# A two-layer decoder trunk on one core: the order of plain and seven-product matmuls in the down projection, the third weight sum, and the place of the gates

## The chip, the cores and the metric

The kernel runs on 1 core of one Trainium2 chip, as one program. The metric is the device time of one execution in microseconds. Three runs of the kernel before gave a median of 2934.0 us (2933.38 to 2938.09).

TensorE (PE) does the matmuls and writes them to PSUM; VectorE (DVE) and ScalarE (ACT) do the elementwise work; GpSimd (POOL) does little here but issue some transfers; SyncE (SP) issues most transfers. Every engine takes its own instructions in the order of the program.

## What is computed

Two decoder layers on 256 tokens of width 2048, in float32. Layer 0 mixes with a gated DeltaNet and a latent attention side by side, layer 1 with retention. Each layer then has a gated feed-forward part with a short convolution, which is where most of this change lies, and a gated embedding:

```python
def conv_ffn(hn, w_up, conv_w, conv_b, w_down):
    u = causal_dwconv(hn @ w_up, conv_w) + conv_b
    gate, up = jnp.split(u, 2, axis=-1)
    return (jax.nn.silu(gate) * up) @ w_down
```

`w_up` is 2048 x 11264 and `w_down` 5632 x 2048. The DeltaNet needs two small gates per token and head, from 16 columns of its input projection:

```python
    beta = jax.nn.sigmoid(b.astype(f32)).transpose(0, 2, 1)
    g = (-jnp.exp(A_log.astype(f32)) * jax.nn.softplus(a.astype(f32) + dt_bias.astype(f32))
         ).transpose(0, 2, 1)
```

## The kernel before

**Split precision.** Every product of two float32 matrices is made of three products of float32r parts: high x high, low x high, high x low. A block of weights is loaded into one of four `raw` buffers of 1 MB (L167). `cut` (L186, L187) makes its high part on ScalarE by a rounding copy, and its low part on VectorE by a subtraction, in halves of 128x1024; there are four buffers each for the high halves (`hi`) and the low ones (`lo`). TensorE then runs the two products with the high part (in a "high step") and the one with the low part (in a "low step"). So a weight passes SyncE, ScalarE, VectorE and TensorE in turn, and every stage can only be as far ahead as it has buffers.

**The feed-forward part.** The 44 blocks of 128 hidden units are taken in groups: 4, then five groups of 8. For a group, `up` makes the hidden units (`gemm_b`, L259 and L264, 48 steps for a group of 8), convolves and gates them, and leaves them split in tiles `xg`. `down` multiplies a finished group with its rows of `w_down` and adds the result to the residual `h`. `down` of one group runs while `up` of the next one does: both are generators that give up their turn at each `yield`, and `ffn` takes 6 steps of `up` (`LAG`), and from then on 0.9 steps of `down` (`SHARE`) for one of `up`.

**The two ways of `down`.** The output has 2048 columns, four blocks of 512. For the first and the last group all four are plain matrix products (`gemm_a`, L288, L289 and L294): 6 steps a block, 24 matmuls of 512 columns for each load of 1 MB. For the four groups between, columns 1024 to 2047 are plain (12 steps), and columns 0 to 1023 are done by `seven`: tokens, hidden units and these 1024 columns are halved each, so that hidden units, weights and results fall into four quarters, and the four quarters of the result come from seven products of sums of quarters instead of eight products of quarters. There are four such groups in each layer, eight in all, and 56 products.

**One product** (`product`, L423, L424 and L428) has 3 steps: two high steps of 4 matmuls and a low step of 4 + 4. Its left side is a sum of quarters of the hidden units (`Forms`), made ahead on VectorE, or a quarter of them. Its right side is either a quarter of `w_down`, loaded by SyncE into a `raw` buffer (`fresh`), or a sum of two to four quarters. Such a sum is made by the transfers themselves: SyncE writes the first quarter (`put`, L396), and POOL issues a transfer that adds the next one to what is there (`plus`, L400). Both come as two transfers of 512 KB. One running sum, `run_t`, lies in two `xg` tiles of its own and serves three products, with one more quarter added before the second and the third; it can only be added to when the product before has been cast. The other sum, `t3`, the third weight sum of the change's title, lies in a `raw` buffer.

**The order within a group before.** `down` first calls `seven` once, which issues `put` and `plus` for the first running sum. Then come the 12 plain steps, then the 21 steps of the seven products. `t3` is begun after the second product, and used by the sixth. PSUM has four banks for `down` (`pb`): a plain block takes two, and `seven` holds three from its start on.

**Who sets the order.** The program is written with tiles; a scheduler at build time simulates the engines and lays down each engine's order, in general after the order of the text. `tc.issue_after(ins)` ties the instructions written under it behind `ins`, where both are on one engine; `last_cast` is the latest rounding copy of `cut` on ScalarE.

**The gates.** The input projection starts with 3 x 368 columns (`g3` 0 to 2, `gemm_a` with loads of 4 x 368). After the first 368 the 16 gate columns are there; `gates` (L568 to L602) computes `beta` and the decay with small steps on ScalarE and VectorE, among them two loads of a function table on ScalarE. It ends in two small matmuls of cumulative sums (L598, L599). `low_rank` normalises the compressed query, and `rope_tables` (L470 to L495) makes angles on VectorE.

## Time and profile before

| what | us |
|---|---|
| median of three runs | 2934.0 |
| the profiled execution, its time | 2930.12 |
| its span, first to last instruction | 2928.3 |
| PE busy | 2878.1 (98%) |
| DVE busy | 2042.5 (70%) |
| ACT busy | 1532.7 (52%) |
| POOL busy | 141.1 (5%) |

The mean granted clock of TensorE is 0.995 of full speed over the span. The DMA engines moved 570.88 MB, 195 GB/s on average. The page gives busy time of each engine, the chain of work that ended last, and groups of instructions by line, with the idle time ahead of them and what ended it. A group's `x16` is sixteen instructions. In rows of the timeline a bracket like `[1.27 <-ACT hi L186]` says that the engine sat idle for 1.27 us before this instruction, and that ScalarE's instruction of line 186 on a tile `hi` ended it. Rows of windows give, after the window's length, the busy time of PE, PEld (weight loads), DVE, ACT and POOL with the number of instructions, then the granted clock, the mean busy share of the DMA engines and GB/s.

### The profile page before, as it was taken

To read this page: it belongs to the slowest core of one execution; us is meant where nothing else is said; L and a number is where in the kernel's file an instruction comes from. 1 tells how busy PE (TensorE), PEld (TensorE's weight loads), DVE (VectorE), ACT (ScalarE), POOL (GpSimd) and SP (SyncE) were. 2 spreads that over 40 slices of the span, in tenths; PEclk is the share of its full clock that TensorE was granted. 3 is DMA by queue.
4 is the path that set the end of the run, shared out by engine and by line. 5 is a ranking of instruction groups with operands and counts; after the bars stand their busy time and mean duration, and the time that the engine had idled before them with its cause. 6 is when DMAs were issued, how large, how long until landed. Compare 5 with 4: busy or idle time off the path is not lost.

```text
span 2928.3 us, 38655 instructions
## 1 busy us (share of the span) xinstructions
PE 2878.1 (98%) x15076; PEld 2469.8 (84%) x15076; DVE 2042.5 (70%) x2874; ACT 1532.7 (52%) x2185; POOL 141.1 (5%) x132
## 2 busy tenths in 40 slices
PE   8999999999999999999999999999999999999998
PEld 8899988888888888888888888888888887888887
DVE  6878867776868787756665565565677777786865
ACT  6666655554545555554444443444545555555554
POOL 0111100001000000000000000000000000000000
PEclk9999999999999999999999999999999999999999
DMA  6444455568778778555555555555556778777854
GB/s 217 137 141 126 127 165 194 187 198 227 228 208 246 216 232 235 182 191 190 177 188 181 194 180 187 183 182 187 185 188 216 219 227 226 219 216 229 235 180 150
DMA packets 414393, 570.88 MB, mean 195 GB/s; under 512 B 11009, under 2 KB 267137, under 8 KB 414209
## 3 DMA queue, kind: packets, MB, share of 16 engines
q1 hardware_dynamic: 393376, 530.05, 55.4%
q0 software_dynamic: 17408, 33.56, 6.7%
q10 hardware_dynamic: 3424, 4.79, 0.5%
q8 instruction: 118, 1.93, 0.3%
q14 instruction: 67, 0.54, 0.1%
HBM read 566.26 MB, written 2.10 MB: 194 GB/s over the span
## 4 chain that ended last, share of the span: by engine, by line
PE 91%; DMA 3%; DVE 3%; ACT 2%; issue 1%; SPq 0%; POOL 0%; ACTq 0%; POOLq 0%; DVEq 0%
PE pa L259 27%; PE pa L264 14%; PE pa L288 10%; PE pa L289 10%; PE pa L294 10%; DMA raw<-in_l_ffn_w_down_dram 3%; PE pb L289 3%; PE pb L288 3%; PE pb L294 3%; PE pb L698 2%; DVE lo L187 1%; PE pb L424 1%; PE pb L423 1%; PE pb L428 1%; ACT hi L186 1%; PE pb L308 1%
## 5 line engine op out<-in xcount | busy, mean ns | idle before, releaser
L187 DVE TENSOR_TENSOR lo<-raw,hi 128x1024 fp32r<-128x1024 f32 (+3 forms) x1140 | 1194.2, 1075 | 605.2 <-ACT hi L186 493.1
L186 ACT CAST hi<-raw 128x1024 fp32r<-128x1024 f32 (+3 forms) x1140 | 1007.8, 930 | 976.6 <-PE pa L289 327.4
L259 PE MATMUL pa<-xg,hi 128*128 128x512 f32 x3840 | 946.9, 393 | 0.0
L259 PEld LDWEIGHTS pa<-xg,hi 128*128 128x128 f32 x3840 | 714.2, 189 | 143.5 <-DVE xg L313 0.3
L288 PE MATMUL pa<-hi,xg 128*128 128x512 f32 (+1 forms) x1348 | 523.3, 388 | 7.2 <-ACT hi L186 7.1
L289 PE MATMUL pa<-hi,xg 128*128 128x512 f32 (+1 forms) x1348 | 520.8, 387 | 0.3 <-DVE xg L313 0.2
L264 PEld LDWEIGHTS pa<-xg,lo 128*128 128x128 f32 x3840 | 490.2, 191 | 16.4
L264 PE MATMUL pa<-xg,lo 128*128 128x256 f32 x3840 | 501.9, 283 | 0.0
L294 PE MATMUL pa<-lo,xg 128*128 128x512 f32 (+1 forms) x1348 | 332.7, 387 | 0.0
L288 PEld LDWEIGHTS pa<-hi,xg 128*128 128x128 f32 x1348 | 253.7, 188 | 56.9 <-ACT hi L186 7.7
L289 PEld LDWEIGHTS pa<-hi,xg 128*128 128x128 f32 x1348 | 253.8, 188 | 49.0 <-DVE xg L313 0.8
L294 PEld LDWEIGHTS pa<-lo,xg 128*128 128x128 f32 x1348 | 249.8, 188 | 47.5
L1033 DVE SCALAR_TENSOR_TENSOR t<-t,fp,t 128x255 f32<-128x255 f32 (+1 forms) x352 | 157.0, 480 | 57.0 <-ACT t L1031 54.2
L1031 ACT ACTIVATE t<-t,fp 128x256 f32<-128x256 f32 x176 | 96.1, 593 | 84.5 <-DVE t L274 84.4
L271 ACT COPY t<-pa 128x512 f32<-128x512 f32 x128 | 74.9, 585 | 117.0 <-PE pa L264 107.6
L289 PE MATMUL pb<-hi,xg 128*128 128x512 f32 x348 | 135.9, 391 | 0.0
L288 PE MATMUL pb<-hi,xg 128*128 128x512 f32 x348 | 135.8, 390 | 0.0
L400 POOL DMA_DIRECT2D xg<-in_l_ffn_w_down_dram x48 | 58.0, 1207 | 1198.3 <-DMA xg<-in_l_ffn_w_down_dram 481.9
L156 POOL TENSOR_TENSOR small<-small,mhalf 128x1 f32<-128x1 f32 (+2 forms) x38 | 28.6, 753 | 1372.1 <-DVE small L1198 622.6
L272 DVE TENSOR_TENSOR t<-t,pa 128x512 f32<-128x512 f32 x128 | 87.0, 680 | 2.2 <-ACT t L271 2.2
L294 PE MATMUL pb<-lo,xg 128*128 128x512 f32 x348 | 86.5, 389 | 0.0
L313 DVE SCALAR_TENSOR_TENSOR xg<-pb,par,xg 128x256 fp32r<-128x256 f32 x136 | 59.8, 479 | 35.8 <-ACT xg L312 35.0
(280 smaller groups left out, 2236.8 us busy)
## 6 DMA issues: line engine op xcount, KB each, us to landing
raw<-in_l_ffn_w_up_dram SPq DMA_DIRECT2D x176, 1024.0 KB, 5.2
raw<-in_l_w_in_dram SPq DMA_DIRECT2D x128, 1024.0 KB, 5.1
raw<-in_l_ffn_w_down_dram SPq DMA_DIRECT2D x56, 1024.0 KB, 5.2
raw<-in_l_w_out_dram SPq DMA_DIRECT2D x44, 1024.0 KB, 5.1
raw<-in_l_ffn_w_down_dram SPq DMA_DIRECT2D x64, 512.0 KB, 5.9
raw<-in_l_ple_gate_dram SPq DMA_DIRECT2D x32, 1024.0 KB, 5.1
xg<-in_l_ffn_w_down_dram POOLq DMA_DIRECT2D x48, 512.0 KB, 7.1
xg<-in_l_ffn_w_down_dram SPq DMA_DIRECT2D x16, 512.0 KB, 6.6
```

The lines of the kernel that those rows point to most:

```text
L186: last_cast[0] = A.copy(vo(hi)[:, c], vi(rk)[:, c])
L187: V.tensor_sub(vo(lo)[:, c], vi(rk)[:, c], vo(hi)[:, c].bitcast(F32))
L259: last_mm[0] = T.matmul(ps[:, j], wh, x2, start=first, stop=False)
L264: last_mm[0] = T.matmul(ps[:, j, :S], lo[k][:, j * P : (j + 1) * P], xr(tiles, c * 8 + k)[1], start=False, stop=c == 1 and k == 7)
L271: A.copy(u, ps[:, :, S:])
L272: V.tensor_add(u, u, ps[:, :, :S])
L288: T.matmul(o[i], xh, hi[k], start=begin and k0 + k == 0, stop=False)
L289: last_mm[0] = T.matmul(o[i], xw, hi[k], start=False, stop=False)
L294: last_mm[0] = T.matmul(o[i], xl(tiles, k0 + k, i)[0], lo[k], start=False, stop=end and k0 + k == nkb - 1)
L313: V.scalar_tensor_tensor(t[:, kk, 1], pk, g, t[:, kk, 0].bitcast(F32), op0=ALU.mult, op1=ALU.subtract)
L1031: A.activation(y[:, j], u[:, j], AF.Identity, scale=fc(ct + 176), bias=fc(ct + 264))
L1033: V.scalar_tensor_tensor(y[:, j, lag:], u[:, j, : S - lag], fc(ct + (2 - lag) * 88), y[:, j, lag:], op0=ALU.mult, op1=ALU.add)
```

## The change

There are four edits.

- `down` takes plain products and the seven products in turns over the whole group: one plain step, two steps of `seven`, and so on. `seven` is still called once ahead for its first sum. `SHARE` goes from 0.9 to 0.85.
- In `seven` the product of `left(0)` is no longer kept in PSUM to have the fourth product added: it is subtracted from `h12` by itself, one more subtraction on VectorE for each group. Two banks are in use at a time instead of three.
- `t3` is begun after the fourth product instead of the second.
- `gates` and `low_rank(cq)` are tied behind the last cast on ScalarE.

```diff
--- before.py
+++ after.py
@@ -32,7 +32,7 @@
 PSA = 2
 PSB = 4
 LAG = 6
-SHARE = 0.9
+SHARE = 0.85
 RATES = [1.7, 1.1, 1.1, 0.95, 2.8]
 D = 2048
 S = 256
@@ -433,27 +433,32 @@
         put(run_t, 0, 0)
         plus(run_t, 0, 1)
         yield
-        A_, B_, C_ = pb(), pb(), pb()
-        yield from product(C_, forms.left(0), run_t, True)
-        V.tensor_sub(h22, h22, C_)
+        one = pb()
+        yield from product(one, forms.left(0), run_t, True)
+        V.tensor_sub(h22, h22, one)
+        V.tensor_sub(h12, h12, one)
         plus(run_t, 1, 1)
-        yield from product(A_, x(0, 0), fresh(0, 0), True)
-        V.tensor_add(h11, h11, A_)
+        acc = pb()
+        yield from product(acc, x(0, 0), fresh(0, 0), True)
+        V.tensor_add(h11, h11, acc)
+        one = pb()
+        yield from product(one, x(1, 0), fresh(1, 0), True)
+        V.tensor_add(h11, h11, one)
+        yield from product(acc, forms.left(1), run_t, False)
+        V.tensor_sub(h12, h12, acc)
+        plus(run_t, 1, 0)
         t3 = slab()
         put(t3, 0, 1)
         plus(t3, 1, 1)
-        yield from product(B_, x(1, 0), fresh(1, 0), True)
-        V.tensor_add(h11, h11, B_)
-        yield from product(A_, forms.left(1), run_t, False)
-        V.tensor_sub(h12, h12, A_)
-        plus(run_t, 1, 0)
-        yield from product(C_, forms.left(3), fresh(1, 1), False)
-        V.tensor_sub(h12, h12, C_)
-        yield from product(A_, forms.left(2), t3, False)
-        V.tensor_sub(h22, h22, A_)
-        V.tensor_add(h21, h21, A_)
-        yield from product(B_, x(1, 1), run_t, True)
-        V.tensor_add(h21, h21, B_)
+        one = pb()
+        yield from product(one, forms.left(3), fresh(1, 1), True)
+        V.tensor_sub(h12, h12, one)
+        yield from product(acc, forms.left(2), t3, False)
+        V.tensor_sub(h22, h22, acc)
+        V.tensor_add(h21, h21, acc)
+        one = pb()
+        yield from product(one, x(1, 1), run_t, True)
+        V.tensor_add(h21, h21, one)
 
     def put_split(t, k, n, src):
         A.copy(t[:, k : k + n, 0], src)
@@ -620,8 +625,9 @@
             nc.sync.dma_start(cst, a["cst"][:, :N_CST])
             V.tensor_copy(posf, posi)
         if g3 == 2:
-            gates()
-            low_rank(cq)
+            with tc.issue_after(last_cast[0].ins):
+                gates()
+                low_rank(cq)
             cqT = []
             later(lambda: None, lambda: None, lambda: cqT.extend(gained(cq, C_QN)))
             rope_tables(cst[:, C_IMLA : C_IMLA + 1], cos_t, sin_t, cst[:, C_SIGN : C_SIGN + 1])
@@ -1050,16 +1056,26 @@
 
         def down(g0, g1, tiles, forms):
             r0, nk = g0 * P, g1 - g0
-            if forms is not None:
-                fast = seven(w_dn, r0, 0, tiles, forms)
-                next(fast)
-            for c in range(0 if forms is None else 2, CG):
-                ps = [pb() for _ in range(NH)]
-                yield from gemm_a(w_dn, r0, nk, c * 512, 512, tiles, ps)
-                for i in range(NH):
-                    V.tensor_add(h[i][c], h[i][c], ps[i])
-            if forms is not None:
-                yield from fast
+
+            def plain(cols):
+                for c in cols:
+                    ps = [pb() for _ in range(NH)]
+                    yield from gemm_a(w_dn, r0, nk, c * 512, 512, tiles, ps)
+                    for i in range(NH):
+                        V.tensor_add(h[i][c], h[i][c], ps[i])
+
+            if forms is None:
+                yield from plain(range(CG))
+                return
+            fast = seven(w_dn, r0, 0, tiles, forms)
+            next(fast)
+            slow = plain(range(2, CG))
+            while next(slow, fast) is not fast:
+                yield
+                for _ in range(2):
+                    if next(fast, slow) is not slow:
+                        yield
+            yield from fast
 
         groups = [(max(g - 4, 0), g + 4) for g in range(0, NFT, 8)]
         prev = None
```

What the build makes of it at three places follows (tile names with their numbers; a number tells one buffer's content from another).

**The gates, on ScalarE**, behind the copies out of the first 368 columns (L547 before, L552 now). `small` tiles are the gates', `hi` are halves of weights. Before:

```order
L547 ACTIVATE slab_79<-pa_15_144,small_58_378 128x16
L547 ACTIVATE t2_61_383<-pa_15_144,small_58_378 128x352
L569 ACTIVATE small_89_561<-small_89_561 128x16
L574 ACTIVATE small_90_566<-small_90_566 128x16
L581 ACTIVATE small_93_574<-small_92_572 128x16
L590 ACT_TABLE_LOAD
L590 ACTIVATE small_97_583<-small_94_576 128x16
L594 ACT_TABLE_LOAD
L594 ACTIVATE small_98_587<-alog_388 128x8
L186 CAST hi_68_403<-raw_67_401 128x368 x2
L186 CAST hi_70_409<-raw_67_401 128x368 x2
L186 CAST hi_75_445<-raw_74_443 128x368 x2
```

Now:

```order
L552 ACTIVATE slab_79<-pa_15_144,small_58_378 128x16
L552 ACTIVATE t2_61_383<-pa_15_144,small_58_378 128x352
L186 CAST hi_68_403<-raw_67_401 128x368 x2
...
L186 CAST hi_87_527<-raw_84_519 128x368 x2
L574 ACTIVATE small_89_561<-small_89_561 128x16
L579 ACTIVATE small_90_566<-small_90_566 128x16
L586 ACTIVATE small_93_574<-small_92_572 128x16
L186 CAST hi_109_643<-raw_108_641 128x368
L595 ACT_TABLE_LOAD
L595 ACTIVATE small_97_583<-small_94_576 128x16
L599 ACT_TABLE_LOAD
L599 ACTIVATE small_98_587<-alog_388 128x8
```

The seven gate instructions, two table loads among them, stood ahead of the casts of the next two loads (`hi_68` to `hi_87`), and stand behind them now.

**The first product of the first group, on ScalarE and TensorE.** `xg_1186` and `xg_1187` are the running sum, `raw_1190` the first plain load, `raw_1195` (before) and `raw_1198` (now) the next load of `up`. ScalarE before:

```order
L186 CAST hi_1193_6565<-raw_1190_6559 128x1024
L380 CAST t2_1159_6386<-t2_1157_6380 128x512
L380 CAST t2_1160_6387<-t2_1158_6381 128x512
L271 COPY t2_1178_6513<-pa_1167_6428 128x512
L186 CAST hi_1196_6603<-raw_1195_6601 128x1024
L186 CAST hi_1198_6607<-raw_1195_6601 128x1024
L1031 ACTIVATE t2_1179_6517<-t2_1178_6513,fp_949_4995 128x256 x2
```

ScalarE now:

```order
L186 CAST hi_1193_6565<-raw_1190_6559 128x1024
L380 CAST t2_1159_6386<-t2_1157_6380 128x512
L380 CAST t2_1160_6387<-t2_1158_6381 128x512
L271 COPY t2_1178_6513<-pa_1167_6428 128x512
L1037 ACTIVATE t2_1179_6517<-t2_1178_6513,fp_949_4995 128x256 x2
L186 CAST hi_1196_6594<-xg_1186_6551 128x1024
L186 CAST hi_1199_6604<-raw_1198_6602 128x1024
```

TensorE at the same place, behind the first plain high step and the low step of `up` (L264), before:

```order
L264 MATMUL pa_1180_6524<-xg_932_4913,lo_1185_6532 128x256 x2
L264 MATMUL pa_1180_6524<-xg_934_4923,lo_1185_6532 128x256 x2
L288 MATMUL pb_1189_6558<-hi_1191_6561,xg_1015_5426 128x512
L289 MATMUL pb_1189_6558<-hi_1191_6561,xg_1015_5426 128x512
L288 MATMUL pb_1189_6558<-hi_1191_6561,xg_1015_5426 128x512
```

and now:

```order
L264 MATMUL pa_1180_6524<-xg_932_4913,lo_1185_6532 128x256 x2
L264 MATMUL pa_1180_6524<-xg_934_4923,lo_1185_6532 128x256 x2
L423 MATMUL pb_1195_6593<-hi_1196_6594,t2_1099_5978 128x512
L424 MATMUL pb_1195_6593<-hi_1196_6594,t2_1101_5980 128x512
L423 MATMUL pb_1195_6593<-hi_1196_6594,t2_1099_5978 128x512
L424 MATMUL pb_1195_6593<-hi_1196_6594,t2_1101_5980 128x512
L259 MATMUL pa_1180_6524<-xg_942_4958,hi_1199_6604 128x512 x2
```

Where the second plain high step stood (L288, `hi_1191`), the first product now stands (L423, `hi_1196`), and its cast, which reads the running sum, stands ahead of the casts of the next load of `up`. All eight groups have the product at this place.

**SyncE's queue.** Around the writes of the running sum (`xg`), before:

```order
L167 DMA raw_1195_6601<-in_l0_ffn_w_up_dram 128x8x256
L167 DMA raw_1200_6635<-in_l0_ffn_w_down_dram 128x4x512
L167 DMA raw_1209_6694<-in_l0_ffn_w_up_dram 128x8x256
L396 DMA xg_1186_6551<-in_l0_ffn_w_down_dram 128x2x512
L396 DMA xg_1187_6552<-in_l0_ffn_w_down_dram 128x2x512
L167 DMA raw_1216_6732<-in_l0_ffn_w_down_dram 128x4x512
```

and now:

```order
L167 DMA raw_1198_6602<-in_l0_ffn_w_up_dram 128x8x256
L167 DMA raw_1209_6681<-in_l0_ffn_w_up_dram 128x8x256
L396 DMA raw_1215_6712<-in_l0_ffn_w_down_dram 128x2x512
L396 DMA xg_1186_6551<-in_l0_ffn_w_down_dram 128x2x512
L396 DMA xg_1187_6552<-in_l0_ffn_w_down_dram 128x2x512
L396 DMA raw_1215_6712<-in_l0_ffn_w_down_dram 128x2x512
L167 DMA raw_1218_6747<-in_l0_ffn_w_up_dram 128x8x256
```

The two writes stand behind the same number of 1 MB loads as before; half of the second product's block (`raw_1215`) is now ahead of them and half behind, where a whole load of `up` was ahead. Around the third sum, before (`raw_1276` is the third sum, `raw_1277` the next product's block):

```order
L396 DMA raw_1251_6982<-in_l0_ffn_w_down_dram 128x2x512 x2
L167 DMA raw_1264_7024<-in_l0_ffn_w_up_dram 128x8x256
L167 DMA raw_1271_7078<-in_l0_ffn_w_up_dram 128x8x256
L396 DMA raw_1276_7097<-in_l0_ffn_w_down_dram 128x2x512 x2
L396 DMA raw_1277_7102<-in_l0_ffn_w_down_dram 128x2x512 x2
L167 DMA raw_1285_7161<-in_l0_ffn_w_up_dram 128x8x256
L167 DMA raw_1294_7224<-in_l0_ffn_w_up_dram 128x8x256
```

and now (`raw_1280` is the third sum, `raw_1282` the next product's block):

```order
L167 DMA raw_1261_6988<-in_l0_ffn_w_up_dram 128x8x256
L167 DMA raw_1268_7046<-in_l0_ffn_w_up_dram 128x8x256
L167 DMA raw_1275_7080<-in_l0_ffn_w_down_dram 128x4x512
L396 DMA raw_1280_7117<-in_l0_ffn_w_down_dram 128x2x512 x2
L396 DMA raw_1282_7123<-in_l0_ffn_w_down_dram 128x2x512 x2
L167 DMA raw_1288_7146<-in_l0_ffn_w_up_dram 128x8x256
L167 DMA raw_1295_7204<-in_l0_ffn_w_up_dram 128x8x256
```

Third sum and next block stand side by side in both; now a plain load (`raw_1275`) is in the stretch ahead of them, and the block of the second product (`raw_1251` before) has gone.

## The prediction

> **What bounds the kernel now.** I read the page first, then the waits, then the stages around the change.
>
> ```profile
> span 2928.3 us, 38655 instructions
> PE 2878.1 (98%) x15076; PEld 2469.8 (84%) x15076; DVE 2042.5 (70%) x2874; ACT 1532.7 (52%) x2185; POOL 141.1 (5%) x132
> PE 91%; DMA 3%; DVE 3%; ACT 2%; issue 1%; SPq 0%; POOL 0%; ACTq 0%; POOLq 0%; DVEq 0%
> ```
>
> TensorE is the bound: 2878 of 2928 us busy, 91% of the chain. The change takes no matmul away, so it can only win or lose idle time of PE, and time in which PE works at a lower clock. The list of waits shows what idle there is (columns: us in total, times, longest us):
>
> ```profile
> PE pb L428 <- DVE lo L187: 18.4, 15, 1.8
> PE pb L423 <- ACT hi L186: 7.6, 9, 1.3
> PE pa L288 <- ACT hi L186: 7.1, 2, 5.4
> ```
>
> The first two, 18.4 + 7.6 = 26.0 us, are the seven products waiting for their split weights. The third is almost wholly one wait of 5.4 us at the start, behind the gates. The eight stretches of 22 us that hold the products' waits, one per group, say the same, and add the clock:
>
> ```profile
> 724.00:746.00 22.00, 17.89 (x73) 13.93 (x73) 15.82 (x24) 11.37 (x15) 2.18 (x2) 0.84 0.83 239
> ...
> 996.00:1018.00 22.00, 18.53 (x87) 14.93 (x87) 16.64 (x25) 12.85 (x17) 2.41 (x2) 0.92 0.88 248
> ...
> 2443.00:2465.00 22.00, 17.80 (x81) 13.95 (x80) 16.56 (x24) 11.82 (x15) 1.21 (x2) 0.92 0.82 245
> 2580.00:2602.00 22.00, 18.14 (x86) 14.52 (x85) 16.20 (x25) 12.59 (x16) 1.87 (x2) 0.92 0.86 247
> ...
> sum 176.00, PE 150.02 PEld 120.71 DVE 135.70 ACT 101.13 POOL 16.58; mean PE 18.75 PEld 15.09 DVE 16.96 ACT 12.64 POOL 2.07
> ```
>
> PE is busy 150.0 of 176 us: again 26.0 us idle. The granted clock is 0.84 in one stretch and 0.92 in three (the four left out show 1.00), which is (0.16 + 3 x 0.08) x 22 = 8.8 us more. So **about 35 us is all that evening out the groups can give back**. How idle turns into a low clock is seen in the first stretch (PE's timeline, then two windows of all engines):
>
> ```profile
> 727.09 0.50 PE L423 MATMUL pb<-hi,xg 128*128 128x512 f32 x1 [1.27 <-ACT hi L186]
> ...
> 734.88 0.73 PE L428 MATMUL pb<-lo,xg 128*128 128x512 f32 x2 [1.83 <-DVE lo L187]
> 736.62 1.22 PE L428 MATMUL pb<-lo,xg 128*128 128x512 f32 x2 [1.00 <-DVE lo L187]
> 737.64 3.62 PE L259 MATMUL pa<-xg,hi 128*128 128x512 f32 x8
> ```
>
> ```profile
> 732.00:736.00 4.00, 1.79 (x11) 1.15 (x10) 4.00 (x7) 3.81 (x5) 0.00 (x0) 0.96 0.39 125
> 736.00:740.00 4.00, 3.38 (x8) 2.71 (x9) 4.00 (x6) 1.69 (x3) 0.00 (x0) 0.50 0.51 147
> ```
>
> After 1.83 and 1.00 us of idle close together the clock is 0.50, and eight matmuls that take 2 us elsewhere take 3.62.
>
> **Why those waits are there.** From SyncE's timeline, the chain in order of time, and the page's table of DMA issues:
>
> ```profile
> 709.34 9.10 SPq L396 DMA_DIRECT2D raw<-in_l_ffn_w_down_dram  x4
> ```
>
> ```profile
> 717.96 10.82 DMA raw<-in_l_ffn_w_down_dram
> ...
> 2710.45 10.46 DMA raw<-in_l_ffn_w_down_dram
> ```
>
> ```profile
> raw<-in_l_ffn_w_down_dram SPq DMA_DIRECT2D x64, 512.0 KB, 5.9
> ...
> raw<-in_l_ffn_w_down_dram POOLq DMA_DIRECT2D x16, 512.0 KB, 9.8
> ```
>
> The four issues from 709.34 on are the third sum's block and the next product's block, side by side. The chain holds eight pieces of 9.9 to 11.1 us for the latter (first and last shown), one per group, against a median of 5.9 for such a load: POOL's accumulates run beside them, and the third sum has taken one of the four `raw` buffers long before its use.
>
> **The change, part by part.** Durations are from the profiled execution, so the sum is made against its 2930.1 us; the median of the runs is 2934.0, 3.9 higher, and I add the same 3.9 at the end.
>
> *Gates.* Rows of before, ScalarE, TensorE and VectorE:
>
> ```profile
> 31.39 0.56 ACT L547 ACTIVATE t<-pa,small 128x352 f32<-128x352 f32 x1
> ...
> 35.43 3.28 ACT L186 CAST hi<-raw 128x368 fp32r<-128x368 f32 x8
> ```
>
> ```profile
> 35.97 0.68 PE L288 MATMUL pa<-hi,xg 128*128 128x368 f32 x1 [5.44 <-ACT hi L186]
> ...
> 40.76 1.51 PE L294 MATMUL pa<-lo,xg 128*128 128x368 f32 x8
> ```
>
> ```profile
> 31.80 0.35 DVE L478 TENSOR_SCALAR t<-posf,slab 128x256 f32<-128x256 f32 x1
> ...
> 36.18 1.89 DVE L187 TENSOR_TENSOR lo<-raw,hi 128x368 fp32r<-128x368 f32 x4
> ...
> 38.31 0.42 DVE L476 SCALAR_TENSOR_TENSOR t<-t,t 128x256 f32<-128x256 f32 x1
> ```
>
> The casts could start at 31.95, behind the copies, instead of 35.43: 3.5 us. But VectorE then has ten angle steps of 0.3 to 0.42 us from 31.80 on, where the gates' steps stood, so its first low parts come at about 35.4, hardly before 36.18. PE gets through its low half (40.76 now) when four of them are done, near 37.3, so 3.5 us earlier at most. The gates' two table loads then stand in front of later casts, with ScalarE up to four tiles ahead: 0 to 2 us are lost again. I take **-3, between -3.5 and 0**.
>
> *Waits inside the groups.* Plain products and products in turns give fewer block loads per us, and the third sum takes its buffer later. The pace of PE follows from one row of the chain:
>
> ```profile
> 158.06 3.65 PE pa L259 x16
> ```
>
> That is 0.228 us a matmul; an up load is 16 of these and 16 of half the columns (1.9 us, the L264 row below), 5.6 us, a plain load 24, 5.4 us, half a product's load 6, 1.4 us. In the new queue the next product's block has 1.4 + 5.6 + 5.4 = 12.4 us from the release of its buffer until its cast comes up, against 1.4 + 5.6 = 7 now, so even 10.8 us is covered. The up load behind it has 6.8 us, and shares the engines with two sums instead of four transfers; ScalarE's lead of a few half loads covers most of what is missing. I leave 5 of the 35: **-30, between -35 and 0** (all of it comes back if the burst has only moved).
>
> *The first product.* This is the term that decides. Its right side is the first weight sum: two SyncE writes, then two POOL accumulates, then a cast. Now twelve plain steps lie ahead of it; after the change one does. The writes stay where they are: in SyncE's queue the load right ahead of them is, before and after, the fourth one behind `raw_1181` and takes over its buffer, so it starts at the same point of the work. Rows of the first group (SyncE, POOL, TensorE), and of the last:
>
> ```profile
> 655.56 1.09 SPq L396 DMA_DIRECT2D xg<-in_l_ffn_w_down_dram  x2
> ...
> 662.34 1.37 POOL L400 DMA_DIRECT2D xg<-in_l_ffn_w_down_dram  x1 [166.63 <-DMA xg<-in_l_ffn_w_down_dram]
> ```
>
> ```profile
> DMA to landing us min/median/max: 5.7/7.1/9.1
> ```
>
> ```profile
> 663.11 2.08 PE L264 MATMUL pa<-xg,lo 128*128 128x256 f32 x16
> 665.03 0.40 PE L288 MATMUL pb<-hi,xg 128*128 128x512 f32 x1
> ```
>
> ```profile
> 2648.10 1.04 SPq L396 DMA_DIRECT2D xg<-in_l_ffn_w_down_dram  x2
> ...
> 2657.52 0.40 PE L288 MATMUL pb<-hi,xg 128*128 128x512 f32 x1
> ```
>
> In the new order of PE the first product stands exactly where L288 stands at 665.03, 9.5 us after the writes were issued (9.4 in the last group). When is its cast done? The accumulate starts at 662.34 now; in front of the writes stands half a load instead of a whole one, so say 661.4. It lands 7.1 to 7.7 us later (median of all 48; of this group's first two, 7.7), at 668.5 to 669.1; the cast of 128x1024 takes 1.05:
>
> ```profile
> 656.55 1.05 ACT L186 CAST hi<-raw 128x1024 fp32r<-128x1024 f32 x1
> ```
>
> PE goes on at about 669.8: **4.8 us of idle, in each of the eight groups**. By the ends of the row, 5.7 and 9.1 with the accumulate at 661.4 and 662.3, it is 3.1 and 7.5. Nothing can hide it: PE, ScalarE and POOL work in order, and ScalarE's next casts, of the up load, stand behind this one. PE then restarts at a low clock; the rows above cost 1.8 (0.08 x 22) to 3.5 us (0.16 x 22) for shorter idle, and I take 2. No further wait follows, since four slow matmuls (1.8 us by the row at 737.64) outlast a cast of 1.05. So 8 x 6.8 = **+54, between 25 (3.1, clock kept) and 88 (7.5 and 3.5)**.
>
> The Trainium skill, in "TensorE: Matmul & The Clock Gate", Part 1, says that the array falls to half clock after an idle window of about 3.4 us and comes back after 3.4 us of work. By that rule a late sum costs 1.7 us of clock, and the term would be 8 x 6.5 = 52, an estimate from that page. The trace agrees with the half, 0.50, but shows it after 1.83 and 1.00 us with work between, so I keep the rows.
>
> *The rest* costs nothing. Eight more subtractions on VectorE are 8 x 0.68 us:
>
> ```profile
> 714.56 0.68 DVE L438 TENSOR_TENSOR t<-t,pb 128x512 f32<-128x512 f32 x1
> ```
>
> VectorE is 70% busy; if that cover were gone they would cost 5.4 us. PSUM has four banks for two plain outputs, one held and one short-lived product, and a bank has a whole other step to come free. The second use of the running sum has two products of cover, and the third sum some 30 us of PE for its 5.9 + 9.8 us of transfers. The share of 0.85 instead of 0.9 ends the 33 steps of a group at up step 6 + 33 / 0.85 = 45 of 48 instead of 43.
>
> **Sum:** 2930.1 - 3 - 30 + 54 = 2951.1 in the profile, 2955 in the runs: slower by 0.7%. With the terms' middle errors (gates -3.5 to -1, groups -35 to -22, first product 41 to 69, which is 5.1 to 8.6 a group) it lies between 2936 and 2980.
>
> **The rivals.**
>
> *A. The sum is hardly late.* If the writes land with the first half load and the accumulate takes its least, and the clock stays up, the term is about 8 x 3.6 = 29: 2934 - 3 - 30 + 29 = 2930, no change. For it: 3.1 us is the low end of the rows. Against it: 1.83 and 1.00 us were already enough to halve the clock, and the transfers run in a stretch that is busy with DMA.
>
> *B. Faster: the first product doesn't wait.* It decides if the first sum is cast by 665, that is, lands within 2.6 us of the accumulate's start; then 2934 - 3 - 35 = 2896. For it: the build's order assumes it. Against it: the least of 48 landings is 5.7 us.
>
> *C. The burst only moves.* Third sum and next block still stand side by side in SyncE's queue, with the second half of the running sum between them on POOL. If the waits inside the groups stay whole, the sum is 2934 - 3 + 54 = 2985. For it: the transfers are the same. Against it: nearly twice the time ahead of the block that was late.
>
> **How the numbers follow.** A measurement of this kernel tells about 0.2%, 6 us, from no change. Forecast 0.60 (2955), A 0.16, B 0.10, C 0.14. Faster: B and a quarter of A, and little of the forecast's low end, 0.15. Same: the rest of A and the low end of the forecast, 0.16. Slower: 0.69. The range 2920 to 2986 leaves out B and half of C; the forecast's own is 2936 to 2980.
>
> **What would show it.** Right: PE's L423 waiting on ScalarE's cast for 3 to 7 us eight times, each first in its group, some 10 us after the writes, with a clock near 0.5 behind it; the wait of 5.4 us at the start down to about 2; the eight long pieces of the chain gone from the middle of the groups and DMA or POOL pieces in their place at its start. Wrong: no wait of L423 over 2 us at a group's start (B), or clock 1.00 behind it (A), or waits of L428 on VectorE still near 18 us (C).

## The result and the profile after

The changed kernel takes **3046.9 us** (median of 4 runs, 3045.7 to 3052.9) against 2933.7 us, a ratio of 1.0386 (95% interval 1.0368 to 1.0404). It is slower by 113 us; the forecast was slower by 21, and the range ended at 2986. The profiled execution took 3052.9 us. Its page:

```profile
span 3051.1 us, 38714 instructions
...
PE 2925.1 (96%) x15076; PEld 2489.3 (82%) x15076; DVE 2054.3 (67%) x2882; ACT 1540.0 (50%) x2185; POOL 141.3 (5%) x132
```

The same number of matmuls, but PE stands idle for 126 us instead of 50, and is busy for 47 us longer, most of it because it works longer at a low clock. The list of waits says where (us in total, times, longest):

```profile
ACT hi L186 <- DMA raw<-in_l_ffn_w_up_dram: 87.7, 17, 9.5
...
ACT hi L186 <- DMA xg<-in_l_ffn_w_down_dram: 58.5, 8, 8.0
...
PE pb L423 <- ACT hi L186: 55.0, 8, 7.6
...
PE pa L259 <- ACT hi L186: 45.6, 8, 7.6
...
PE pa L288 <- ACT hi L186: 5.0, 3, 2.0
```

There are **two stalls in each of the eight groups**. L423 is the first product, waiting for the running sum: it was forecast. L259 is a high step of `up` some 83 us after the sum's writes, waiting for its weights: it was not. The 18.4 us of L428 are gone from the head of the list. The chain of waits of the first group shows both (start, us, what):

```profile
663.88 8.53 DMA xg<-in_l_ffn_w_down_dram
...
672.52 1.05 ACT hi L186
...
673.61 0.80 PE pb L423
...
675.69 1.71 PE pa L259 x4
...
678.25 3.49 PE pa L259 x12
681.74 0.23 PE pb L288
...
734.29 10.62 DMA raw<-in_l_ffn_w_up_dram
...
744.99 1.05 ACT hi L186
...
746.09 2.08 PE pa L259 x4
748.16 0.43 PE pb L288
```

Behind each stall matmuls of 0.23 us take 0.43. The windows of that stretch give the granted clock (the column behind the engines' busy times):

```profile
673.60:675.60 2.00, 1.99 (x5) 1.60 (x6) 2.00 (x2) 1.44 (x2) 0.48 (x1) 0.50 0.22 39
...
677.60:679.60 2.00, 2.00 (x6) 1.59 (x5) 0.00 (x0) 0.00 (x0) 0.00 (x0) 0.50 0.91 159
679.60:681.60 2.00, 2.00 (x10) 1.58 (x10) 0.00 (x0) 0.75 (x1) 0.00 (x0) 0.98 0.43 78
```

Here the clock is 0.50 until 679.6, for 6.0 us of work, which costs 3.0 us. Read in windows of 0.25 us, the sixteen stalls differ: the low clock lasts for 2.9 to 6.2 us of work and costs 1.5 to 3.1 us, 20.7 us behind the eight waits of L423 and 21.7 behind the eight of L259. So over the eight groups the first stall costs 55.0 + 20.7 = 76 us and the second 45.6 + 21.7 = 67. Less the 35 us that the groups of the kernel before lost, that is 108 of the 123 us between the two spans. Counted by kind, the 123 us are 76 of idle, 36 of low clock (47 against 11 us, by windows of 1 us over both spans) and 11 of PE time that is busy at an unchanged clock, of which more below.

### The profile page after: what moved, and what is told of

Its sections match the earlier page's. It is cut to its first block, busy times and chain, and to the rows that moved or that the text cites. A ratio compares the mean times of both kernels' runs of the same rounds, so it can differ in the third digit from the quotient of the medians.

```text
span 3051.1 us, 38714 instructions
## 1 busy us (share of the span) xinstructions
PE 2925.1 (96%) x15076; PEld 2489.3 (82%) x15076; DVE 2054.3 (67%) x2882; ACT 1540.0 (50%) x2185; POOL 141.3 (5%) x132
## 4 chain that ended last, share of the span: by engine, by line
PE 86%; DMA 7%; DVE 4%; ACT 2%; issue 1%; POOL 0%; ACTq 0%; POOLq 0%; SPq 0%; DVEq 0%
PE pa L259 26%; PE pa L264 13%; PE pa L288 10%; PE pa L294 10%; PE pa L289 10%; DMA xg<-in_l_ffn_w_down_dram 3%; DMA raw<-in_l_ffn_w_up_dram 3%; DVE lo L187 2%; PE pb L289 2%; PE pb L288 2%; PE pb L294 2%; PE pb L423 2%; PE pb L704 2%; PE pb L424 1%; ACT hi L186 1%
## 5 line engine op out<-in xcount | busy, mean ns | idle before, releaser
L259 PE MATMUL pa<-xg,hi 128*128 128x512 f32 x3840 | 975.4, 400 | 45.6 <-ACT hi L186 45.6
L259 PEld LDWEIGHTS pa<-xg,hi 128*128 128x128 f32 x3840 | 724.5, 193 | 200.2 <-ACT hi L186 54.4
L288 PE MATMUL pa<-hi,xg 128*128 128x512 f32 (+1 forms) x1348 | 524.2, 389 | 5.1 <-ACT hi L186 5.0
L264 PEld LDWEIGHTS pa<-xg,lo 128*128 128x128 f32 x3840 | 495.0, 191 | 33.0 <-DVE lo L187 13.0
L264 PE MATMUL pa<-xg,lo 128*128 128x256 f32 x3840 | 514.6, 284 | 0.2
L288 PEld LDWEIGHTS pa<-hi,xg 128*128 128x128 f32 x1348 | 254.4, 189 | 55.0 <-ACT hi L186 5.9
L288 PE MATMUL pb<-hi,xg 128*128 128x512 f32 x348 | 139.8, 402 | 0.0
L289 PE MATMUL pb<-hi,xg 128*128 128x512 f32 x348 | 139.6, 401 | 0.0
L187 DVE TENSOR_TENSOR lo<-xg,hi 128x1024 fp32r<-128x1024 f32 x48 | 58.0, 1223 | 84.9 <-ACT hi L186 61.9
L423 PE MATMUL pb<-hi,t 128*128 128x512 f32 x128 | 57.1, 446 | 55.0 <-ACT hi L186 55.0
L186 ACT CAST hi<-xg 128x1024 fp32r<-128x1024 f32 x48 | 49.5, 1047 | 88.4 <-DMA xg<-in_l_ffn_w_down_dram 58.5
```

The source lines that it names most:

```text
L186: last_cast[0] = A.copy(vo(hi)[:, c], vi(rk)[:, c])
L187: V.tensor_sub(vo(lo)[:, c], vi(rk)[:, c], vo(hi)[:, c].bitcast(F32))
L259: last_mm[0] = T.matmul(ps[:, j], wh, x2, start=first, stop=False)
L264: last_mm[0] = T.matmul(ps[:, j, :S], lo[k][:, j * P : (j + 1) * P], xr(tiles, c * 8 + k)[1], start=False, stop=c == 1 and k == 7)
L288: T.matmul(o[i], xh, hi[k], start=begin and k0 + k == 0, stop=False)
L289: last_mm[0] = T.matmul(o[i], xw, hi[k], start=False, stop=False)
```

## The experiments

All times are medians in us; a ratio stands against the kernel before on the same chip (its median was 2933 to 2936 in every set), with its 95% interval.

| run | us | ratio |
|---|---|---|
| gates_back | 3044.3 | 1.0374 (1.0356 to 1.0391) |
| early_sum | 3047.3 | 1.0386 (1.0370 to 1.0401) |
| t3_as_before | 3052.6 | 1.0401 (1.0386 to 1.0417) |
| no_turns | 2952.5 | 1.0061 (1.0046 to 1.0076) |
| sum_first | 2988.3 | 1.0179 (1.0163 to 1.0194) |
| no_plus3 | 2990.9 | 1.0187 (1.0167 to 1.0207) |
| sum3_later | 3049.4 | 1.0388 (1.0373 to 1.0404) |
| t3_own | 3011.3 | 1.0253 (1.0236 to 1.0271) |
| turns_mid | 2932.4 | 0.9997 (0.9987 to 1.0007) |
| turns_mid_raw5 | 2929.0 | 0.9980 (0.9971 to 0.9989) |
| mid_no_turns | 2931.9 | 0.9989 (0.9979 to 0.9999) |
| turns_share9 | 2937.0 | 1.0012 (1.0003 to 1.0022) |
| **before_mid** | **2893.3** | **0.9864 (0.9849 to 0.9878)** |
| before_mid_raw5 | 2894.4 | 0.9866 (0.9852 to 0.9881) |
| mid_gates | 2893.6 | 0.9862 (0.9847 to 0.9877) |
| mid_share | 2910.8 | 0.9925 (0.9904 to 0.9947) |
| mid_front | 2905.4 | 0.9905 (0.9891 to 0.9920) |

### Which edit carries the loss

**No turns** (`yield from plain(range(2, CG))`, then `yield from fast`):

> The changed kernel with the plain products all ahead of the seven again (share of 0.85, later third sum, new banks and gates kept). Theory (the turns cost the first stall, the later third sum the second): the first stall goes, about 74 us, the second stays in part: 2950 to 2980 us. Rival 1 (the turns make both stalls, the third sum's place is harmless without them): 2905 to 2940 us. Rival 2 (the later third sum makes both): about 3047 us.

2952.5 us, inside the first theory's range. L423 no longer waits; L259 still does:

```profile
PE pa L259 <- ACT hi L186: 43.5, 8, 7.4
```

So the turns make the first stall, and the second stands without them. What is left of the change here is the third sum's new place, and the share, the banks and the gates.

**The third sum behind the second product again**, turns kept:

> The changed kernel with the third sum begun behind the second product, as before, all else as changed. Theory (the second stall of a group, 4.9 to 7.8 us idle and 2 to 3 us of low clock some 83 us behind the first writes, comes from the third sum's writes and accumulates standing next to the next product's block and the accumulates of the running sum): it shrinks or goes, 2980 to 3005 us. Rival (the up loads are late because one of four load buffers is held by the third sum, and it is now held longer): no gain or a loss, 3045 us or more.

3052.6 us: neither came out. The second stall did not go and did not stay, it moved with the sum, and begins at 716.0 in the first group. The chain there:

```profile
705.65 14.86 DMA raw<-in_l_ffn_w_up_dram
```

The up load behind the third sum's block and the next product's now lands in 14.86 us. Behind the second product (now) and behind the fourth (in the change) a product's block is due next, and in both places the load behind the two is late.

**The gates back in front of the casts:**

> The changed kernel with the gates put back in front of the casts; all else as changed. In the changed kernel's trace TensorE's first wait there fell from 5.4 to 1.9 us, but waits of 1.1 and 2.8 us came 20 us later. Theory (the gates are worth nothing, what came later paid it back): 3045 to 3049 us, the 5.4 us wait back and the later two gone. Rival (the prediction's -3 is there and hidden by other losses): 3050 us or more.

3044.3 us, 0.7 below the theory's range, with runs (3043.4 to 3050.0) that overlap the changed kernel's. The wait of 5.4 us is back and the wait of L308 is gone, as the theory said. The cleaner test comes at the end.

### The first stall

**The first sum begun earlier in the text**, at the start of the group:

```diff
+            yield
...
+                if prev[3] is not None:
+                    next(behind_it)
                 for _ in range(LAG):
                     next(going)
```

> The changed kernel with the first running sum (two writes, two accumulates) issued at the start of a group, six up steps (two up loads, about 11 us of TensorE) earlier; nothing else moves. Theory (the first product waits only because its sum is begun 11 us too late): the eight waits of 6.3 to 7.7 us and the slow matmuls behind them, about 9.2 us a group, go; 3047 - 74 = 2973 us, between 2965 and 2990. Rival (products in turns ask for more transfers than the queues can land, so the lateness moves to the next load): above 3025 us, with an equal wait at another place of the first 40 us of a group.

3047.3 us, and the waits of L423 are 52.5 us. This is no verdict on either theory, since the scheduler put the writes back where they had been. SyncE's timeline of this run:

```profile
658.30 0.37 SPq L396 DMA_DIRECT2D raw<-in_l_ffn_w_down_dram  x1
658.73 0.97 SPq L396 DMA_DIRECT2D xg<-in_l_ffn_w_down_dram  x2
659.74 0.52 SPq L396 DMA_DIRECT2D raw<-in_l_ffn_w_down_dram  x1
```

The two writes (`xg`) still stand between the halves of the second product's block, at 658.7 (657.65 in the changed kernel).

**The writes held ahead in the queue:** each of the next eight loads is traced in `load` under `tc.issue_after` of the second write.

```diff
+            if sums[1] > 0:
+                sums[1] -= 1
+                s.enter_context(tc.issue_after(sums[0].ins))
+            for q in range(0, k, k // parts):
...
-        put(run_t, 0, 0)
+        sums[:] = put(run_t, 0, 0), 8
```

> The changed kernel with one thing held fast: the loads written behind the first running sum may not be put ahead of its two writes in SyncE's queue, so the writes stand three loads earlier (in the second group behind the load issued at 791, not behind the one at 801). Theory (the first product's wait is only the place of the writes in that queue): the waits of 6.3 to 7.7 us with the low clock behind them, about 9.2 us a group, go: 3047 - 74 = 2973 us, between 2965 and 2990. Rival (the landings are slow whatever the place, some load is late in any case): above 3020 us.

2988.3 us, 58.6 less. SyncE's timeline, and the list of waits of TensorE:

```profile
636.62 1.09 SPq L401 DMA_DIRECT2D xg<-in_l_ffn_w_down_dram  x2
```

```profile
PE pa L264 <- ACT hi L191: 46.6, 8, 7.9
...
PE pb L293 <- ACT hi L191: 10.0, 6, 1.7
```

(Lines are five higher here: L264 is L259, L293 is L288.) The writes go at 636.6, the waits of L423 are gone, and the second stall is untouched. A small new wait took some of the gain: 10.0 us at the first plain product. It is measured by itself below.

### The second stall

SyncE and POOL in the changed kernel, behind the fourth product of the first group:

```profile
720.91 7.09 SPq L396 DMA_DIRECT2D raw<-in_l_ffn_w_down_dram  x4
734.29 6.84 SPq L167 DMA_DIRECT2D raw<-in_l_ffn_w_up_dram  x2
```

```profile
723.80 1.19 POOL L400 DMA_DIRECT2D xg<-in_l_ffn_w_down_dram  x1 [33.39 <-DVE lo L187]
725.50 2.44 POOL L400 DMA_DIRECT2D raw<-in_l_ffn_w_down_dram  x2 [0.50 <-DMA raw<-in_l_ffn_w_down_dram]
730.22 1.19 POOL L400 DMA_DIRECT2D xg<-in_l_ffn_w_down_dram  x1 [2.28 <-issue]
```

Eight transfers of 512 KB within 9.3 us (720.91 to 730.22): the third sum's two writes and two accumulates, the next block's two pieces, and the running sum's last two accumulates. The up load comes at 734.29 on top. The DMA queues from 720 to 745 (packets, MB, share of the time of 16 engines):

```profile
q0 software_dynamic: 1088, 2.10, 48.8%
q1 hardware_dynamic: 2775, 3.81, 47.2%
```

**The engines are full**, 96%, and POOL's accumulates take half of it for a third of the bytes.

That alone makes no stall. In the kernel before, the same eight transfers go out within 11.2 us (706.75 to 717.96), the engines are 99% busy from 709 to 734, and the up load behind the burst lands in 12.46 us, 11.7 to 13.3 in the eight groups. SyncE's timeline there, and the landing of this one load:

```profile
719.32 6.91 SPq L167 DMA_DIRECT2D raw<-in_l_ffn_w_up_dram  x2
```

```profile
DMA to landing us min/median/max: 12.5/12.5/12.5
```

No L259 waits for it, because its first matmul stands at 737.64, 18.3 us behind the issue. In the changed kernel TensorE stands still 6.1 us behind the issue (746.09 less its wait of 5.69, less 734.29). So the stall takes both, a slow landing and a short lead. The next runs change the one or the other.

**Without the third sum's accumulates:** `plus(t3, 1, 1)` left out, so that the sixth product multiplies one block instead of a sum of two.

> The changed kernel without the two accumulates of the third sum, which then holds one block in place of two; all else is done. Theory (the up load that stalls the second time is slow, 10.6 us, because the third sum's accumulates land beside it): it lands in 6 to 8 us, and the second stall of about 8.6 us a group falls to 0 to 4 us: 2980 to 3010 us. Rival (that load is issued too late, since the third sum holds one of four load buffers): the stall stays above 4 us of idle, 3030 us or more.

2990.9 us. The same 25 us of this run (722 to 747), its chain there, and its waits:

```profile
q1 hardware_dynamic: 3168, 4.19, 49.6%
q0 software_dynamic: 544, 1.05, 27.3%
```

```profile
736.29 6.86 DMA raw<-in_l_ffn_w_up_dram
```

```profile
PE pa L259 <- ACT hi L186: 5.7, 6, 1.9
```

The load lands in 6.86 us in place of 10.62, and the waits of L259 fall from 45.6 to 5.7 us: the theory of the burst.

**The third sum in two buffers of its own:** `t3` in two `xg` tiles (`XB` 20, `T2B` 23).

> The changed kernel with the third sum in two buffers of its own beside the running sum's, so that all four load buffers stay with the loads; paid for with four of the 27 small work buffers of 2 KB. Theory of the burst: the same transfers stand side by side, the second stall stays above 4 us of idle: 3030 to 3050 us. Theory of the buffer (the third sum holds one of four, so the up load is issued only 6 us before it is due): the second stall goes, about 69 us, 2975 to 2995 us.

3011.3 us, between the theories. SyncE's timeline, its chain, and its list of waits:

```profile
725.48 0.37 SPq L167 DMA_DIRECT2D raw<-in_l_ffn_w_up_dram  x1
725.90 1.32 SPq L396 DMA_DIRECT2D xg<-in_l_ffn_w_down_dram  x2
```

```profile
732.73 13.19 DMA raw<-in_l_ffn_w_up_dram
```

```profile
PE pa L264 <- DVE lo L187: 23.1, 6, 4.2
```

With all four buffers for loads, one up load goes out ahead of the third sum's writes: the load that stalled in the changed kernel, at 725.48 instead of 734.29, which is 7.2 us earlier in the group (this run is 1.6 us ahead by then, by the plain load in front: 711.82 against 713.37). It lands in 6.01 us, and no L259 waits any more. The load behind it is now the one beside the third sum's accumulates. It takes 13.19 us; ScalarE stands still at its cast, VectorE's next low part comes behind that, and TensorE waits in six low steps. So lead and landings both have a part: 56 us without the accumulates, 36 us with the buffers.

**The running sum's last accumulates later in the text**, behind the fifth product:

> The changed kernel with the running sum's last pair of accumulates begun behind the fifth product, not beside the third sum. If the burst at the end of the fourth product is what makes the up load slow: two of its six pieces go, the second stall falls by 2 to 4 us a group, 3015 to 3030 us. If the load is late for want of a buffer: no change, 3045 to 3050 us.

3049.4 us, and again a text edit that the scheduler undid. POOL's timeline:

```profile
723.94 1.19 POOL L400 DMA_DIRECT2D xg<-in_l_ffn_w_down_dram  x1 [33.44 <-DVE lo L187]
725.32 1.19 POOL L400 DMA_DIRECT2D raw<-in_l_ffn_w_down_dram  x1 [0.18 <-issue]
```

The running sum's piece still goes ahead of the third sum's, so this run tells nothing.

### The third sum behind the third product

The fourth product takes the running sum and asks SyncE for no block. A third sum begun just ahead of it has no block beside it:

```diff
+        t3 = slab()
+        put(t3, 0, 1)
+        plus(t3, 1, 1)
         yield from product(acc, forms.left(1), run_t, False)
...
-        t3 = slab()
-        put(t3, 0, 1)
-        plus(t3, 1, 1)
```

With the turns and the writes held ahead, and then with a fifth load buffer too:

> The changed kernel with the writes of the first running sum three loads earlier (as in the run before) and the third sum begun behind the third product, one product earlier: the fourth product takes the running sum and asks SyncE for nothing, so in SyncE's queue two up loads and a plain load now stand between the third sum's block and the next product's. Theory of the burst (accumulates beside the next block make the up load late): the second stall falls from about 8.6 to 0 to 3 us a group: 2988 - 45 = 2943 us, between 2925 and 2955. Theory of the buffer (the third sum holds one of four load buffers, and now longer): no gain, 2985 us or more.

> The run above with a fifth load buffer, paid for with four of the 27 small work buffers. Theory of the burst: hardly more to win than what is left of the waits, 0 to 20 us under the run above. Theory of the buffer: all of the second stall goes only here, 2920 to 2940 us, and 45 us or more under the run above.

2932.4 and 2929.0 us. The first loses the second stall, 56 us under `sum_first` (L264 is L259 here):

```profile
PE pa L264 <- ACT hi L191: 4.8, 6, 1.8
```

The fifth buffer is worth 3 us. The up load that stalled in `sum_first` has no more lead than there: it goes at 727.08 instead of 728.42, in a run that is 1.3 us ahead by then. But it lands in 5.13 us instead of 10.55. So here it is the burst and not the buffer. The loads that now stand behind the burst are still slow (10.47 us for the one at 706.18), and come early enough. But with both stalls gone, the change is only back at the time of the kernel before. The same single edit in **the kernel before**, alone and with the fifth buffer:

> The kernel before with one edit, the third sum begun behind the third product in place of the second. The 40 us that its groups lose were put down to the third sum's and the next product's blocks side by side in SyncE's queue; here they stand apart. If that holds: 2934 - 25 = 2909 us, between 2900 and 2925. If those waits come from the products in a row alone: 2930 to 2938 us.

> The run above with a fifth load buffer, paid for with four of the 27 small work buffers. If a load's lead is what is short: what is left of the 40 us goes, 2895 to 2905 us. If not: as the run above, or up to 10 us slower for the four small buffers.

**2893.3 us, ratio 0.9864**, more than was expected, and 2894.4 with the buffer. The page and what is left of TensorE's waits for weights:

```profile
span 2893.0 us, 38659 instructions
...
PE 2867.5 (99%) x15076; PEld 2467.3 (85%) x15076; DVE 2041.3 (71%) x2874; ACT 1531.6 (53%) x2185; POOL 141.3 (5%) x132
```

```profile
PE pa L288 <- ACT hi L186: 7.8, 2, 5.4
```

L423 and L428 no longer appear, and L259 waits 0.3 us once. So the 35 us which the change set out to win were lost to the third sum's place, not to plain products and products standing in a row. By which way is not separated here: the third product's block, for which the kernel before waited, now stands ahead of the third sum, so it goes out 8.2 us earlier (711.94 against 717.54, in a run that is 2.6 us later by then) and also lands in 5.8 to 7.3 us instead of 8.4 to 10.8. This version beats both kernels.

### What the other edits cost

`turns_mid` is 39 us over `before_mid`. Three runs say which edits that is:

> The run of 2932 us (first writes earlier, third sum behind the third product) with the plain products all ahead of the seven again; gates, banks, share and the held order of the writes stay. If the turns themselves cost what is left: 2893 to 2900 us. If the other edits do: 2925 to 2935 us.

2931.9 us: taking the turns away does not change the time at this share. But two things cancel in it. PE in the pages of `turns_mid` (span 2929.8 us) and of this run (2931.7 us):

```profile
PE 2889.5 (99%) x15076; PEld 2459.2 (84%) x15076; DVE 2053.6 (70%) x2882; ACT 1541.3 (53%) x2185; POOL 141.2 (5%) x132
```

```profile
PE 2880.1 (98%) x15076; PEld 2473.0 (84%) x15076; DVE 2051.4 (70%) x2882; ACT 1532.6 (52%) x2185; POOL 141.6 (5%) x132
```

With turns PE is idle for 40 us instead of 52, and loses 5 us to the low clock instead of 14 (windows of 1 us): they do even out the group. But PE is busy for 9 us longer over the same matmuls although it loses 9 us less to the clock, so the mixed order costs it some 18 us. They show as short gaps: taking 0.2265 us from the start of a matmul of 512 columns to the next start as usual, and 0.1195 for 256 columns, what goes beyond by less than 0.2 us adds up to 58.2 us with turns and 40.5 without. Why the mixed order has more of them was not tested.

So one edit each was added to `before_mid`, the share of 0.85 and the held writes:

> The run of 2893 us (the kernel before, third sum behind the third product) with the share of 0.85 in place of 0.9. By the ledger of the run without turns, whose groups lose about 31 us of which eight waits of 1.7 us with their clock (15 us) stand at the first plain product: the share costs the rest, 2893 + 15 to 25 = 2908 to 2918 us. By the prediction it costs nothing: 2890 to 2896 us.

> The run of 2893 us with the first running sum's writes held ahead of the loads written behind them. If the early accumulates make the two loads beside them late (9 to 10 us in place of 5) and so cost the 1.7 us wait at the first plain product in each group: 2893 + 15 = 2908 us. If not: 2890 to 2896 us.

2910.8 (+17.5) and 2905.4 us (+12.2); with 2893.3 that makes 2923 of the 2931.9, and 9 us are left to the banks and to edits acting together, which was not separated. With the share of 0.85 one up load in place of two stands between the blocks of the second and third product in SyncE's queue, and L259 waits again, for the up load behind the third sum and its neighbour (in the first group it takes 13.24 us, and 8.00 in `before_mid`):

```profile
PE pa L259 <- ACT hi L186: 16.1, 7, 4.5
```

With the writes held ahead, TensorE shows the wait that `sum_first` had:

```profile
665.36 0.50 PE L293 MATMUL pb<-hi,xg 128*128 128x512 f32 x1 [1.67 <-ACT hi L191]
```

**Turns with the share of 0.9:**

> The run of 2932 us with turns, with the share of 0.9. If the share costs only where the products stand in a row: 2928 to 2936 us. If it costs here too: 2908 to 2920 us.

2937.0 us, 1 us above the first range, and 4.6 more than with 0.85. At 0.9 the nearest kernel without turns is `mid_front` at 2905.4, so here the turns (with the banks) cost some 30 us: PE is busy for 2894.4 us instead of 2868.2, and there is less idle for them to even out. At 0.85 they cost nothing on balance. In no pair of runs did they win.

**The gates alone**, on `before_mid`:

> The run of 2893 us (the kernel before, third sum behind the third product) with the gates queued behind the casts, as in the change. The prediction's term: 3 us faster, 2889.5 to 2893. Against it, from the trace of the changed kernel, where two later waits of 1.1 and 2.8 us took the place of 3.6 us won: 2892 to 2896 us.

2893.6 against 2893.3 us (2892.4 to 2895.1 against 2891.6 to 2894.8): no difference that these runs show. In the changed kernel's timeline of TensorE one sees why:

```profile
34.29 0.47 PE L288 MATMUL pa<-hi,xg 128*128 128x368 f32 x1 [1.86 <-ACT hi L186]
...
55.34 0.43 PE L288 MATMUL pa<-hi,xg 128*128 128x368 f32 x1 [1.11 <-ACT hi L186]
...
62.47 0.69 PE L308 MATMUL pb<-ident,t 128*128 128x128 f32 x2 [2.83 <-DVE t L617]
```

The wait of 5.4 us is down to 1.86, and the delayed gates and `low_rank` come up later as 1.11 and 2.83: 5.8 us in all.

## Why the prediction was right or wrong

**Gates, -3: wrong by 3.** The first wait fell as forecast. The step that failed is the one that gave the later casts "0 to 2 us" and did not ask who waits for `low_rank`: its transposes (L308) do. The runs show no gain: the term is 0.

**First product, +54: right in mechanism, too small.** L423 waits first in each group, eight times, at half the clock. In the first group the writes go at 657.65, PE is through its low step at 667.3 (673.61 less its wait of 6.34), 9.6 us later as forecast, and the sum lands 14.8 us behind the writes, where 12.9 to 13.5 were assumed: the accumulate takes 8.5 us, not 7.1 to 7.7, with the second product's block and an up load issued right around it. So the idle is 6.9 us on average, not 4.8, and that is the size that was missed. The clock costs 2.6 us on average where 2 were taken. The term measures 76 in the trace, within its range of 25 to 88; taking the wait away gave 58.6, with 10 us of new waits and their clock against it. The Trainium skill's page "TensorE: Matmul & The Clock Gate", Part 1, has the clock back after about 3.4 us of sustained work. By an estimate from that figure a stall would cost 1.7 us of clock. The trace decides: behind the sixteen stalls the clock came back after 2.9 to 6.2 us of work, 5.3 on average.

**Waits inside the groups, -30: wrong in sign, and the heart of the miss.** The prediction read the cause of the old waits rightly, third sum and next block side by side, and then priced the cure by the pace of TensorE alone. The step that failed is "The up load behind it has 6.8 us, and shares the engines with two sums instead of four transfers; ScalarE's lead of a few half loads covers most of what is missing." The load had 6.1 us, took 10.62, and ScalarE had no lead to give. The burst had not become lighter either: eight transfers in 9.3 us now, eight in 11.2 us before. The price could be read in the kernel before, whose up load behind the burst took 12.46 us. It was covered there only by its lead of 18.3 us, and the new order cut this lead to a third. The term is 67 - 35 = +32 instead of -30, 62 us from the forecast. Rival C had the right mechanism, "The burst only moves", but as a limit took the old 35 us: the burst moved in front of a load with less lead, and cost nearly twice as much.

**"The rest costs nothing": wrong for the share.** It was looked at only for where a group ends (step 45). It also sets which load stands between which blocks, and costs 17.5 us in the old order (`mid_share`). Nor is the order of the matmuls free for PE: with turns it is busy for some 18 us more at the same clock (`turns_mid`).

Together: +3, +22 and +62 against the three terms make 87 of the 102 us by which the profiled execution (3052.9) is above the 2951.1 that was forecast for it; the runs came out 92 above their forecast. Of the 15 us left, some 11 are the busy time at an unchanged clock, and the rest is not located. **The direction** was right for a reason that held, the first product's wait. Rivals A and B fell with it: no wait of L423 was short, and none kept its clock.

## What to carry to other kernels

When transfers that are issued together make a load late, the victim is the load behind them. Price the new place of the burst by that load: how long before its use it is issued, against how long a load beside such a burst takes to land (here 10.6 to 13.3 us, and the trace of the kernel before had the figure), not by the time until the burst itself is needed. Look first for a place where nothing else is due: here a shift of three lines by one product gave 1.4%, and the reordering of the whole group no gain. And before a run on a scheduled program is read, look whether the queue's order changed at all: two text edits here did not move a single transfer.

## What was not expected of the hardware

- POOL's accumulating transfers take 48.8% of the engines' time for 2.10 MB and SyncE's 47.2% for 3.81 MB in the same 25 us: 1.9 times as long a byte. The loads of 1 MB shown above beside them landed in 10.6 to 14.9 us, where the median of the changed kernel's 176 up loads is 5.6:

```profile
raw<-in_l_ffn_w_up_dram SPq DMA_DIRECT2D x176, 1024.0 KB, 5.6
```

- The clock, once at 0.50, came back after 2.9 to 6.2 us of unbroken matmuls in the sixteen stalls of one execution, 2.6 us lost a stall on average, where the prediction took 2.
